# A hybrid four-mixer layer on one core: 44 transfers issued from GpSimd instead of ScalarE

## The chip, the cores and the metric

The kernel runs on one core of one Trainium2 chip. The metric is the device time in microseconds of one execution; the time before is the median of three runs. The engines are TensorE (PE in the profile, PEld for its weight loads), VectorE (DVE), ScalarE (ACT), GpSimd (POOL) and SyncE (SP). Transfers are issued from the queues of SyncE, ScalarE or GpSimd, and the same 16 DMA engines carry all of them.

## The reference

One pre-norm layer on x of 1 x 512 x 1024, float32. The input is normalised, multiplied with a combined input projection, and split into four causal token mixers of width 256 and four sets of gates:

```python
h = _rmsnorm(x, norm1_g)
proj = h @ w_in
p_gdn, p_lru, p_s5, p_rwkv, p_gate = _split(proj, (GDN_COLS, LRU_COLS, S5_COLS, RWKV_COLS, GATE_COLS))
ys = (_gdn_mixer(p_gdn, ...), _rglru_mixer(p_lru, ...), _s5_mixer(p_s5, ...), _rwkv7_mixer(p_rwkv, ...))
for i in range(N_BRANCH):
    term = jax.nn.sigmoid(gate_logits[:, :, i]) * (ys[i] @ w_branch[i])
    merged = term if merged is None else merged + term
x = x + (merged @ w_out).astype(x.dtype)
h2 = _rmsnorm(x, norm2_g)
x = x + (jnp.square(jax.nn.relu(h2 @ mlp_w1)) @ mlp_w2).astype(x.dtype)
```

A final norm closes it. Gated DeltaNet (GDN) and RWKV-7 are computed in chunks of 64 tokens, each with 4 heads; for both, a unit triangular 64 x 64 matrix has to be inverted for each of the 8 chunks and 4 heads. S5 is a diagonal complex recurrence over groups of 16 channels.

## The kernel before, in words

Every large product is made of three float32r products: each operand is split into a rounded part (hi) and the rest (lo). Weights come in units of 128 x 1024 (`unit`, line 316): SyncE loads `raw` (line 313), ScalarE makes hi (line 333), VectorE makes lo (line 334, which the profile shows as line 120 with tile lo). `proj` (line 415) is one 128 x 512 tile of the projection, 24 matmuls, tile acc.

The mixers are written as steps, and PLAN (line 68) lists them: among others rwkv_a, s5_a, s5_b, gdn_l, gdn_k, rwkv_b, s5_y, rwkv_i, gdn_b, gdn_i, rwkv_r, gdn_r, and between them the gates ga_10 to ga_31. After them come `merge` and `mlp`, which hold about half of the time. Each step runs at a priority level (LV, line 62). The order of instructions on each engine is then fixed at build time by a planner (`schedule_with_timeline_sim=True`, line 1834), which lays them out on a timeline of its own, by priority and by when their inputs are ready. Each engine works through its list in order. So the order on the engines follows from the engine that each instruction is given to, as well as from its place in the code. Buffers in SBUF are handed out by `al` (line 138) from a table of places (HOME), in the order of the code.

The places where ScalarE issues transfers:

- `tri_inverse` (line 444), run once for RWKV (scratch scrr) and once for GDN (scrg). The 16 pairs of 64 x 64 matrices are written to DRAM (line 448), read back as 128 groups of 16 x 16 diagonal blocks into `nb` (line 452), inverted there by VectorE in 15 steps (lines 457 to 461), written out as `tn` and its transpose `tm` (line 468) and read back in the matrix layout as `a0t` and `tf` (line 472). Each of the four exchanges is half SyncE's and half ScalarE's: two transfers (lines 448, 452) or four (468, 472). At 448 and 452 the halves are two parts of one tile, at 468 and 472 the first of a pair (tn, a0t) is SyncE's and the second (tm, tf) ScalarE's. TensorE then assembles the full inverse in the matmuls zp, t1p, t2p, z2p and z3p (tiles zpr to z3pr and zpg to z3pg): zp reads a0t, t1p reads tf. Each ScalarE transfer here has 1024 contiguous runs, of 64 or 256 bytes.
- `rwkv_a` (line 617): four transfers of 512 runs from kr to ab.
- `gdn_b` (line 864): four broadcast loads of 1024 runs from gscr into gr and br, beside four of SyncE's into eg.
- `s5_b` (line 1297): eight loads of 256 runs from scu into ug, read by the matmuls s5v.
- `s5_y` (line 1355): sixteen loads of 128 runs from scy into yf, which is then added, put through a GELU (ScalarE) and read by the matmuls glu.

These are 12, 4, 4, 8 and 16, together 44. ScalarE also issues four stores of the output in `finish` (line 1654). GpSimd issues 24 weight loads that add to what is there (lines 330 and 332), all after 350 us, and does the memsets.

Of the kernel before, what the change touches and what calls it, by code (L numbers as in the profile page):

```python
# [100 lines left out]
def trunk(ctx, tc, order, xT, wall, w8, prm, big, cst, gfr, out):  # L101
# [342 lines left out]
    def tri_inverse(nt, tf, nm):  # L444

        scr = tri_scr[nm]
        for par in range(2):
            (nc.sync, nc.scalar)[par].dma_start(
                out=flat(scr, 4160 * par, [[64, 64], [8320, 16], [1, 64]]), in_=nt[64 * par:64 * par + 64])
        nb, tn, tn2, tmp = (t1(n + nm) for n in ("nb", "tn", "tm", "tp"))  # L450
        for qe in range(2):
            (nc.sync, nc.scalar)[qe].dma_start(
                out=v3(nb, 16)[64 * qe:64 * qe + 64], in_=flat(scr, 1040 * qe, [[2080, 64], [64, 16], [1, 16]]))
        nb3, tn3, tm3, tp3 = v3(nb, 16), v3(tn, 16), v3(tn2, 16), v3(tmp, 16)
        V.memset(tn, 0.0)
        V.memset(tn[:, 0:256:17], 1.0)
        for j in range(14, -1, -1):
            n = 15 - j
            tt(V, tp3[:, 0:n, 0:n], tn3[:, j + 1:16, j + 1:16],
               nb3[:, j:j + 1, j + 1:16].to_broadcast([128, n, n]), MUL)  # L460
            V.tensor_reduce(out=tn3[:, j + 1:16, j:j + 1], in_=tp3[:, 0:n, 0:n], axis=AX.X, op=ADD)
        V.tensor_copy(out=tm3, in_=tn3.rearrange("p c r -> p r c"))
        fr(nb, tmp)
        t0t = t4("t0t" + nm)
        a0t = v3(t0t, 16)
        for qe in range(2):
            for s, t in ((0, tn3), (1, tm3)):
                (nc.sync, nc.scalar)[s].dma_start(
                    out=flat(tri_scr[nm, s], 1040 * qe, [[2080, 64], [64, 16], [1, 16]]), in_=t[64 * qe:64 * qe + 64])
        for par in range(2):  # L470
            for s, t in ((0, a0t), (1, tf)):
                (nc.sync, nc.scalar)[s].dma_start(
                    out=t[64 * par:64 * par + 64], in_=flat(tri_scr[nm, s], 4160 * par, [[64, 64], [8320, 16], [1, 64]]))
        fr(tn, tn2)


        zt, z2 = t4("zt" + nm), t2("z2" + nm)
        G.memset(zt, 0.0)
        zt3, z23 = v3(zt, 16), v3(z2, 16)
        hm = c_("hm")  # L480
        zp = ps("zp" + nm)
        zp4 = v4(zp, 16, 2)
        def pairs(t, x, r0, o):
            return t[r0:r0 + 64, x, :].rearrange("p (b c) -> p b c", b=2)[:, :, o:o + 16]
        for x in range(16):
            for r0 in (0, 64):
                mm(zp4[r0:r0 + 64, x], nt[r0:r0 + 64, x, :], pairs(a0t, x, r0, 0))
        for b in range(4):
            r0, c0 = 32 * b, 32 * (b % 2)
            if b % 2:  # L490
                ts(V, zt3[r0:r0 + 32, :, c0:c0 + 16], zp4[r0:r0 + 32, :, 1], hm[r0:r0 + 32, 0:1], MUL)
            else:
                act(zt3[r0:r0 + 32, :, c0:c0 + 16], zp4[r0:r0 + 32, :, 0], ACT.Copy, hm[r0:r0 + 32, 0:1])
        t1p, t2p = ps("t1p" + nm), ps("t2p" + nm)
        t1p4, t2p3 = v4(t1p, 16, 2), v3(t2p[:, 0:256], 16)
        for x in range(16):
            for r0 in (0, 64):
                mm(t1p4[r0:r0 + 64, x], zt3[r0:r0 + 64, x, :], pairs(tf, x, r0, 16))
        for x in range(16):
            for r0 in (0, 64):  # L500
                mm(t2p3[r0:r0 + 32, x, :], tf[r0:r0 + 32, x, 0:32], zt3[r0:r0 + 32, x, 0:16])
        for b in range(4):
            r0, c0 = 32 * b, 32 * (b % 2)
            A.copy(out=tf[r0:r0 + 16, :, c0 + 16:c0 + 32], in_=t1p4[r0:r0 + 16, :, b % 2])
            if b % 2 == 0:
                tt(V, a0t[r0:r0 + 32, :, 0:16], t2p3[r0:r0 + 32], a0t[r0:r0 + 32, :, 0:16], ADD)
        fr(zt)

        z2p, z3p = ps("z2p" + nm), ps("z3p" + nm)
        z2p3, z3p3 = v3(z2p, 16), v3(z3p, 16)  # L510
        for x in range(16):
            for par in range(2):
                r0 = 64 * par
                mm(z2p3[r0 + 32:r0 + 64, x, :], nt[r0:r0 + 32, x, 32:64], a0t[r0:r0 + 32, x, 0:32])
        for par in range(2):
            r0 = 64 * par
            if par:
                V.tensor_copy(out=z2[r0 + 32:r0 + 64], in_=z2p[r0 + 32:r0 + 64])
            else:
                A.copy(out=z2[r0 + 32:r0 + 64], in_=z2p[r0 + 32:r0 + 64])  # L520
        for x in range(16):
            for par in range(2):
                r0 = 64 * par
                mm(z3p3[r0:r0 + 32, x, :], z23[r0 + 32:r0 + 64, x, :], tf[r0 + 32:r0 + 64, x, 32:64])
        for par in range(2):
            r0 = 64 * par
            if par:
                V.tensor_copy(out=tf[r0:r0 + 32, :, 32:64], in_=z3p3[r0:r0 + 32])
            else:
                A.copy(out=tf[r0:r0 + 32, :, 32:64], in_=z3p3[r0:r0 + 32])  # L530

        fr(t0t, z2)
# [16 lines left out]
    def rwkv_a():  # L549
# [31 lines left out]
        for m in range(2):  # L581
            cl = slice(m * 128, m * 128 + 128)
            kf, sig, af, ei, ea = (t2(n) for n in ("kf", "sig", "af", "ei", "eia"))
            wt_ = al("wt", 520)
            wt = wt_.rearrange("p (c t) -> p c t", c=8)
            o = ps("wl")
            mm(o, b_("wup")[0:64, cl], wa[0:64])
            act(sig, o, ACT.Sigmoid, 1.0, p("w0", m))
            o = ps("al")
            mm(o, b_("wup")[64:128, cl], wa[64:128])  # L590
            act(af, o, ACT.Sigmoid, 1.0, p("a0", m))
            V.tensor_tensor_scan(out=sig, data0=reset, data1=sig, initial=0.0, op0=MUL, op1=ADD)
            V.memset(wt[:, :, 0:1], 1.0)
            act(wt[:, :, 1:65], v3(sig, 8), ACT.Exp, -KDEC)
            act(ei, sig, ACT.Exp, KDEC)
            tt(V, ea, ei, af, MUL)
            shifted(kf, 2 + m)
            sq = sig
            act(sq, kf, ACT.Square, p("kk", m))
            o = head_stat(sq, inv, "k")  # L600
            tt(V, ea, o, ea, MUL)

            act(af, af, ACT.Identity, p("ka", m), omu[:, 8 + m:9 + m])
            tt(V, af, af, kf, MUL)
            kp = af
            stt(kr[:, m, :, 0, :], v3(kf, 8), p("kk", m), wt[:, :, 0:64], MUL, MUL)
            stt(yk[:, m, :, 0, :], v3(kf, 8), p("kk", m), v3(ea, 8), MUL, MUL)
            tt(V, yk[:, m, :, 1, :], v3(kp, 8), v3(ei, 8), MUL)
            fr(kf, sig, ei, ea)
            rf, vf = t2("rf"), t2("vf")  # L610
            shifted(rf, m)
            tt(V, kr[:, m, :, 1, :], v3(rf, 8), wt[:, :, 1:65], MUL)
            for q in range(2):
                V.tensor_copy(out=wc[0:64, :, 2 * m + q], in_=wt[64 * q:64 * q + 64, :, 64])
            fr(wt_)
            for q in range(2):
                nc.scalar.dma_start(out=ab[0:64, :, 2 * m + q].rearrange("p c s t -> p c (s t)"),
                                    in_=kr[64 * q:64 * q + 64, m].rearrange("p c s t -> p c (s t)"))

            tt(V, rf, rf, kp, MUL)  # L620
            rb = al("rb", 128)
            act(rb, b64, ACT.Copy, p("rk", m))
            o = ps("bo")
            mm(o, rb, rf)
            fr(rb)
            shifted(vf, 4 + m)
            tt(V, rf, o, vf, MUL)
            bons.append(rf)

            for hf in range(2):  # L630
                o = ps("vT")
                for c in range(4):
                    mm(o[64:128, c * 128:c * 128 + 128], vf[:, (4 * hf + c) * 64:(4 * hf + c) * 64 + 64], cb)
                A.copy(out=sv[64:128, 4 * hf:4 * hf + 4, 2 * m:2 * m + 2, :], in_=v4(o[64:128], 4, 2))
            fr(af, vf)
# [190 lines left out]
    def gdn_b():  # L826
# [34 lines left out]
        for par in range(2):  # L861
            rr = slice(64 * par, 64 * par + 64)
            for s, t in ((0, gr), (1, br)):
                nc.scalar.dma_start(
                    out=v3(t, 16)[rr],
                    in_=scr[s * 16:s * 16 + 16, 64 * par:64 * par + 64].rearrange("(o x) i -> o x i", o=1).to_broadcast([64, 16, 64]),
                )
# [416 lines left out]
    def s5_b():  # L1284
# [9 lines left out]
        ug = t4("s5ug")  # L1294
        uf = scu.rearrange("m (g c) (t n) -> t c (m g) n", c=16, t=8)
        for t in range(8):
            nc.scalar.dma_start(out=v3(ug, 16)[16 * (7 - t):16 * (7 - t) + 16], in_=uf[t])
        ug3 = v3(ug, 16)
        H = t4("s5h")

# [35 lines left out]
    def s5_y():  # L1336
# [15 lines left out]
        yfv = yf.rearrange("p (m t n) -> p m t n", m=2, t=8)  # L1352
        for g in range(16):
            r0 = 16 * (g % 8)
            nc.scalar.dma_start(out=yfv[r0:r0 + 16, g // 8], in_=scy[:, :, g, :].rearrange("t c n -> c t n"))
        for m in range(2):
            sl = slice(m * 512, m * 512 + 512)
            stt(yf[:, sl], up[:, sl], p("sd", m), yf[:, sl], MUL, ADD)
# [481 lines left out]
```

## Time and profile before

| | |
|---|---|
| median of three runs | 871.31 us (868.24 to 874.57) |
| the profiled execution: its own time, its span | 874.06 us, 872.2 us |
| TensorE busy, mean granted clock | 853.8 us (98% of the span), 0.986 |
| VectorE, ScalarE, GpSimd busy | 550.1, 424.0, 28.3 us |
| ScalarE's queue: packets, MB | 23808, 6.16 |
| GpSimd's queue: packets, MB | 3456, 12.58 |

The mixers, with the gates and branches between them, take the span up to 484 us, where the first matmul of merge (oacc) starts; the MLP follows. In a row of the timeline the first two numbers are start and duration, then come engine, line, operation, and the tiles written and read (a tile's name in the trace may be its region, c, c1a or c1b). What stands in square brackets is the idle time of that engine just before the row and what ended it. A busy TensorE can be one whose clock has been lowered: the granted clock stands beside it in the table of stretches. ACTq, SPq and POOLq are the issuing queues; an issue from ScalarE or SyncE isn't counted as busy time of the engine, one from GpSimd is shown as a POOL row.

### The profile page before, as it was taken

The page shows a single profiled execution, that of the slowest core. Times are in us where ns is not written, and L with a number is a line of the kernel's source. Part 1 is how long each engine was busy: PE and PEld are TensorE (multiplying, and loading weights), DVE is VectorE, ACT ScalarE, POOL GpSimd, SP SyncE. Part 2 cuts the span into 40 slices and gives each one's busy share as a digit, 9 for nine tenths or more (in the row PEclk, how much of TensorE's full clock was granted, in tenths as well). Part 3 has the DMA queues.
Part 4 walks back from the last instruction along what each step waited for, and adds up shares of the span by engine and source line. Part 5 has one row for each costly group of instructions (what it writes and reads, how often), then busy time and mean ns, then how long its engine had stood idle before and what let it go on. Part 6 is the DMA issues. An engine that isn't in the chain of part 4 may idle for free.

```text
span 872.2 us, 12503 instructions
## 1 busy us (share of the span) xinstructions
PE 853.8 (98%) x4911; PEld 689.5 (79%) x4911; DVE 550.1 (63%) x978; ACT 424.0 (49%) x596; POOL 28.3 (3%) x40
## 2 busy tenths in 40 slices
PE   8999999999999999999999999999999999999996
PEld 7777877778777777778888788888888888888885
DVE  7899896984587358736655652464437553868553
ACT  7735648644533264434433334765545443644433
POOL 1000000000000000000000000000100110010000
PEclk9999999996999999999999999999999999999999
DMA  8434225276545652434223232557665777463302
GB/s 300 158 104 134 89 98 106 74 167 172 110 136 161 195 170 86 135 96 132 98 96 97 91 121 88 184 146 187 159 196 166 234 177 209 146 142 100 120 25 97
DMA packets 79292, 119.94 MB, mean 138 GB/s; under 512 B 42545, under 2 KB 49393, under 8 KB 79217
## 3 DMA queue, kind: packets, MB, share of 16 engines
q1 hardware_dynamic: 51968, 100.40, 36.2%
q0 software_dynamic: 3456, 12.58, 8.4%
q10 hardware_dynamic: 23808, 6.16, 3.6%
q8 instruction: 38, 0.62, 0.3%
q14 instruction: 22, 0.17, 0.1%
HBM read 103.79 MB, written 13.17 MB: 134 GB/s over the span
## 4 chain that ended last, share of the span: by engine, by line
PE 87%; DVE 5%; DMA 4%; ACT 2%; issue 1%; ACTq 0%; SPq 0%; DVEq 0%
PE acc L114 29%; PE facc L114 20%; PE dacc L114 17%; PE oacc L114 5%; PE bacc L114 5%; PE s5y L114 1%; DVE c L120 1%; PE s L114 1%; DVE lo L120 1%; DVE c L129 1%; DMA c1a<-scrg 1%; DVE c1b L120 1%; DMA scrr<-c1a 1%; PE s1g L114 0%; DMA c<-scrr 0%
## 5 line engine op out<-in xcount | busy, mean ns | idle before, releaser
L114 PE MATMUL acc<-c,hi 128*128 128x512 f32 x864 | 279.2, 402 | 2.0 <-ACT c L117 1.2
L333 ACT ACTIVATE hi<-raw 128x1024 fp32r<-128x1024 f32 x113 | 119.4, 1058 | 233.2 <-PE facc L114 73.6
L120 DVE TENSOR_TENSOR lo<-raw,hi 128x1024 fp32r<-128x1024 f32 x113 | 137.9, 1222 | 101.4 <-ACT hi L333 99.9
L114 PEld LDWEIGHTS acc<-c,hi 128*128 128x128 f32 x864 | 162.0, 190 | 39.1 <-issue 2.8
L114 PE MATMUL acc<-c,lo 128*128 128x512 f32 x432 | 171.9, 399 | 1.5 <-DVE lo L120 1.5
L114 PE MATMUL facc<-c,hi 128*128 128x512 f32 x336 | 103.5, 389 | 0.0
L114 PEld LDWEIGHTS acc<-c,lo 128*128 128x128 f32 x432 | 82.3, 190 | 21.1 <-DVE lo L120 2.4
L114 PEld LDWEIGHTS facc<-c,hi 128*128 128x128 f32 x336 | 63.1, 188 | 13.1
L117 ACT ACTIVATE c<-c 128x512 f32<-128x512 f32 (+5 forms) x101 | 63.9, 638 | 15.1 <-DVE c L120 11.1
L120 DVE TENSOR_TENSOR c<-c 128x16 f32<-128x16 f32 (+8 forms) x125 | 65.2, 536 | 3.7 <-ACT c L117 2.7
L114 PE MATMUL facc<-c,lo 128*128 128x512 f32 x168 | 65.6, 390 | 0.0
L114 PE MATMUL facc<-c,c1a 128*128 128x512 f32 x264 | 62.8, 391 | 0.0
L114 PE MATMUL dacc<-hi,c 128*128 128x512 f32 x176 | 57.4, 389 | 0.0
L114 PEld LDWEIGHTS facc<-c,c1a 128*128 128x128 f32 x264 | 49.3, 188 | 10.2
L117 ACT ACT_TABLE_LOAD x38 | 48.8, 1283 | 7.8 <-DMA c<-scy 4.3
L120 DVE TENSOR_TENSOR c1a<-raw,c1a 128x1024 fp32r<-128x1024 f32 x21 | 25.7, 1223 | 32.5 <-ACT c1a L333 32.4
L120 DVE TENSOR_TENSOR c<-acc,c 128x512 f32<-128x512 f32 x33 | 22.6, 689 | 34.3 <-PE acc L114 32.5
L114 PE MATMUL bacc<-c1a,hi 128*128 128x512 f32 x128 | 40.9, 405 | 0.7 <-DVE c L120 0.7
L333 ACT ACTIVATE c1a<-raw 128x1024 fp32r<-128x1024 f32 x21 | 22.2, 1059 | 36.4 <-PE facc L114 29.0
L114 PE MATMUL oacc<-c,hi 128*128 128x512 f32 x128 | 39.8, 392 | 0.1
L114 PEld LDWEIGHTS dacc<-hi,c 128*128 128x128 f32 x176 | 33.0, 188 | 6.9
L114 PEld LDWEIGHTS facc<-c,lo 128*128 128x128 f32 x168 | 31.5, 188 | 6.5
(398 smaller groups left out, 1193.7 us busy)
## 6 DMA issues: line engine op xcount, KB each, us to landing
raw<-in_wall_dram SPq DMA_DIRECT2D x134, 512.0 KB, 3.4
c<-in_wall_dram POOLq DMA_DIRECT2D x18, 512.0 KB, 5.5
c<-in_wall_dram SPq DMA_DIRECT2D x6, 512.0 KB, 3.2
raw<-in_wall_dram POOLq DMA_DIRECT2D x6, 512.0 KB, 5.7
scg<-c1b SPq DMA_DIRECT2D x11, 256.0 KB, 2.5
c<-scg SPq DMA_DIRECT2D x11, 256.0 KB, 3.9
c1b<-in_xT_dram SPq DMA_DIRECT2D x8, 256.0 KB, 5.5
c<-in_xT_dram SPq DMA_DIRECT2D x8, 256.0 KB, 4.5
```

Source lines behind the costliest of these rows:

```text
L114: P.matmul(out=o, lhsT=l, rhs=r, start=start, stop=stop)
L117: A.activation(out=o, in_=i, func=f, scale=scale, bias=bias)
L120: e.tensor_tensor(out=o, in0=a, in1=b, op=op)
L129: V.scalar_tensor_tensor(out=o, in0=a, scalar=s, in1=b, op0=op0, op1=op1)
L333: high.append(A.activation(out=hi, in_=raw, func=ACT.Copy, scale=1.0, bias=0.0).ins)
```

## The change

`G` is `nc.gpsimd`. At the places named above, every transfer that ScalarE issued is issued from GpSimd; SyncE's halves stay. The data, the shapes, the tiles and all other instructions are the same, and so are the four output stores.

```diff
-            (nc.sync, nc.scalar)[par].dma_start(
+            (nc.sync, G)[par].dma_start(
                 out=flat(scr, 4160 * par, [[64, 64], [8320, 16], [1, 64]]), in_=nt[64 * par:64 * par + 64])
...
-            (nc.sync, nc.scalar)[qe].dma_start(
+            (nc.sync, G)[qe].dma_start(
                 out=v3(nb, 16)[64 * qe:64 * qe + 64], in_=flat(scr, 1040 * qe, [[2080, 64], [64, 16], [1, 16]]))
...
-                (nc.sync, nc.scalar)[s].dma_start(
+                (nc.sync, G)[s].dma_start(
                     out=flat(tri_scr[nm, s], 1040 * qe, [[2080, 64], [64, 16], [1, 16]]), in_=t[64 * qe:64 * qe + 64])
...
-                (nc.sync, nc.scalar)[s].dma_start(
+                (nc.sync, G)[s].dma_start(
                     out=t[64 * par:64 * par + 64], in_=flat(tri_scr[nm, s], 4160 * par, [[64, 64], [8320, 16], [1, 64]]))
...
-                nc.scalar.dma_start(out=ab[0:64, :, 2 * m + q].rearrange("p c s t -> p c (s t)"),
+                G.dma_start(out=ab[0:64, :, 2 * m + q].rearrange("p c s t -> p c (s t)"),
                                     in_=kr[64 * q:64 * q + 64, m].rearrange("p c s t -> p c (s t)"))
...
-                nc.scalar.dma_start(
+                G.dma_start(
                     out=v3(t, 16)[rr],
...
-            nc.scalar.dma_start(out=v3(ug, 16)[16 * (7 - t):16 * (7 - t) + 16], in_=uf[t])
+            G.dma_start(out=v3(ug, 16)[16 * (7 - t):16 * (7 - t) + 16], in_=uf[t])
...
-            nc.scalar.dma_start(out=yfv[r0:r0 + 16, g // 8], in_=scy[:, :, g, :].rearrange("t c n -> c t n"))
+            G.dma_start(out=yfv[r0:r0 + 16, g // 8], in_=scy[:, :, g, :].rearrange("t c n -> c t n"))
```

## The prediction

> **What bounds the kernel now.** I read the page first, then the table of stretches, then the waits of TensorE, then the timeline around each moved transfer.
>
> ```profile
> PE 853.8 (98%) x4911; PEld 689.5 (79%) x4911; DVE 550.1 (63%) x978; ACT 424.0 (49%) x596; POOL 28.3 (3%) x40
> ...
> q0 software_dynamic: 3456, 12.58, 8.4%
> q10 hardware_dynamic: 23808, 6.16, 3.6%
> ```
>
> TensorE is busy for 853.8 of 872.2 us, so 18.4 us of idle time is all that a better order could win from waits. q10 is ScalarE's queue: counted from the code, its 48 transfers hold 23040 contiguous runs, and 16 closing packets for each make the 23808. 44 of them move (the four output stores stay). q0 is GpSimd's: 24 transfers of 128 runs and 16 packets each make 3456.
>
> The stretches (start:end, length, PE busy, PEld, DVE, ACT, POOL, clock, DMA share, GB/s):
>
> ```profile
> 140.00:160.00 20.00, 19.75 (x94) 15.26 (x94) 15.10 (x59) 19.49 (x26) 0.00 (x0) 1.00 0.46 89
> 200.00:220.00 20.00, 18.41 (x129) 16.02 (x129) 9.36 (x17) 9.19 (x15) 0.00 (x0) 0.66 0.74 200
> 220.00:240.00 20.00, 19.05 (x330) 14.95 (x330) 11.20 (x23) 12.72 (x19) 0.00 (x0) 0.91 0.50 102
> 820.00:872.00 52.00, 44.96 (x199) 36.89 (x197) 20.47 (x31) 19.36 (x35) 0.00 (x0) 0.96 0.19 67
> ```
>
> 7.0 of the 18.4 us lie in the last 52 us, where nothing moves. Around the moved transfers little is idle, but one thing costs more than idle time: between 200 and 240 us the granted clock is 0.66 and 0.91, worth up to (0.34 + 0.09) x 20 = 8.6 us.
>
> ```profile
> PE zpr L114 <- DMA c<-scrr: 1.6, 1, 1.6
> ...
> PE acc L114 <- ACT c L117: 1.2, 1, 1.2
> ...
> PE glu L114 <- ACT c L117: 1.0, 1, 1.0
> ...
> PE zpg L114 <- DMA c1a<-scrg: 0.7, 1, 0.7
> ```
>
> These are TensorE's own waits (total us, times, longest). Three hang on the moved code: zpr and zpg on SyncE's half of the inverses' loads, which share the 16 DMA engines with ScalarE's half, and glu, which comes at the end of the S5 output transfers.
>
> **The change part by part.** *ScalarE's side.* It loses 44 issues of 0.3 to 1 us. That frees ScalarE, not TensorE: ScalarE is 49% busy, and the waits above for it are 1.2 and 1.0 us, the second of which is really for the transfers before it. I take 0 (bounds: 0 and a gain of 1.2).
>
> *GpSimd's side.* What does one transfer of many runs cost there? The trace has only transfers of 128 runs (timeline of POOL, group of L330), beside the hardware queues at 128 and at 1024 runs:
>
> ```profile
> L330 POOL DMA_DIRECT2D c<-in_wall_dram x12 | 10.4, 864 | 124.1 <-DVE lo L120 80.9 <-DVE c1a L120 43.2
> 122.65 0.33 SPq L313 DMA_DIRECT2D raw<-in_wall_dram  x1
> 135.14 0.61 ACTq L448 DMA_DIRECT2D scrr<-c1a  x1
> ```
>
> So t, GpSimd's time for one transfer of 1024 runs, lies between 0.86 us (runs are free) and 8 x 0.864 = 6.9 us (all of the 0.864 goes with the runs). The hardware queue grows by 0.61/0.33 = 1.85, which would give 1.6. With ends so far apart I take the geometric mean, 2.4 us. Transfers of 128 runs cost 0.86. The Trainium skill, DMA: Bandwidth & Descriptors, section "Anatomy of one DMA — SWDGE (gpsimd) path", says that one can emit a lot of descriptors before the incremental cost shows up; no row here shows more than 128 runs, and by that rule t would stay near the low end (it has a rival below).
>
> *Early ones: four of 512 runs (L617) and eight of 256 (L1297).* Their data isn't used for long:
>
> ```profile
> 80.73 1.83 ACTq L1297 DMA_DIRECT2D c<-scu  x2
> ...
> 84.42 2.31 ACTq L1297 DMA_DIRECT2D c<-scu  x3
> 104.60 0.98 PE s5v L114 x28
> ...
> 239.87 0.45 PE L114 MATMUL r<-c,c 128*64 128x64 f32 x8
> ```
>
> Issue ends at 86.7 and the reader s5v comes at 104.6, 18 us later. Eight at most of 1.7 us (double of 0.86) from 80.7 end by 95. L617's are read by the recurrence, whose first matmul r comes at 239.9. Cost 0; if s5v came as soon as the data were there, the 8 us from 86.7 to 95 would count.
>
> *First exchange of RWKV's inverse (L448, L452).* One half of the matrix goes out and one half of nb comes back by GpSimd, each 1024 runs, the second after the first has landed. VectorE's recursion (L460) waits for both halves:
>
> ```profile
> 139.66 3.10 DMA c1b<-scrr
> 143.41 0.15 DVE L120 TENSOR_TENSOR c1b<-c,c1b 128x1 f32<-128x1 f32 x1
> 146.51 1.22 DVE L120 TENSOR_TENSOR lo<-raw,hi 128x1024 fp32r<-128x1024 f32 x1
> 148.40 0.69 DVE L120 TENSOR_TENSOR c1b<-c1b,c 128x512 f32<-128x512 f32 x1 [0.67 <-ACT c L117]
> 151.71 0.69 DVE L129 SCALAR_TENSOR_TENSOR c<-c,c1b 128x512 f32<-128x512 f32 x1 [1.66 <-ACT c L117]
> 154.19 0.90 DVE L120 TENSOR_TENSOR c<-c 128x512 f32<-128x512 f32 x3 [0.77 <-ACT c L117]
> ```
>
> Each leg grows by 2.4 - 0.61 = 1.8 us, so nb lands at 142.8 + 3.6 = 146.4 instead of 142.8. The recursion's first step, at 143.4, then waits 3.0 us, and behind it in VectorE's queue stands a lo split that TensorE needs. Later idle time (0.67 + 1.66 + 0.77 = 3.1 us) takes the delay back. TensorE loses between 0 (the planner writes the recursion later into the queue) and 3.0; I take half, **+1.5**.
>
> *Second exchange (L468, L472).*
>
> ```profile
> 191.04 1.19 POOL L478 MEMSET c1b<- 128x1024 f32 x1 [20.08 <-DVE c L461]
> ...
> 191.37 1.54 ACTq L468 DMA_DIRECT2D scrr<-c1b  x2
> 197.89 1.31 SPq L472 DMA_DIRECT2D c<-scrr  x2
> 201.85 0.30 PE L114 MATMUL zpr<-c,c1a 64*64 64x32 f32 x2 [1.59 <-DMA c<-scrr]
> 217.56 0.30 PE L114 MATMUL t1pr<-c,c1b 64*64 64x32 f32 x2
> ```
>
> With what the issues list has from issue to landing (KB each, median us):
>
> ```profile
> c<-scrr ACTq DMA_DIRECT2D x2, 256.0 KB, 7.6
> ...
> scrr<-c1b ACTq DMA_DIRECT2D x2, 64.0 KB, 6.0
> ```
>
> GpSimd's half fills tf, which is first read by t1pr at 217.6. Behind its own issue of about 0.7 us a ScalarE store landed after another 5.3 us and a load after 7.0: 191.4 + 4.8 + 5.3 + 4.8 + 7.0 = 213.3, so 4 us are spare. GpSimd's own list holds memsets only, here that of zt (L478); put behind the two stores it ends by 198, ahead of the zp matmuls whose results go into zt. SyncE's half fills a0t, for which zpr waits 1.6 us; today four transfers go out at once and take 6.5 us. If GpSimd feeds its two over 4.8 us instead of 1.5, SyncE's two get through sooner: **-1.6**, and by the same way **-0.7** at zpg. The half clock that follows I leave as it is: new waits can call such episodes as an old one can.
>
> *S5 output (L1355) and the gates of GDN (L864).*
>
> ```profile
> 217.50 0.81 ACTq L1355 DMA_DIRECT2D c<-scy  x2
> 225.38 4.30 ACTq L1355 DMA_DIRECT2D c<-scy  x9
> 232.17 1.31 ACTq L864 DMA_DIRECT2D c1a<-gscr  x2
> 234.48 0.96 ACTq L864 DMA_DIRECT2D c1a<-gscr  x1
> 234.49 1.98 PE L114 MATMUL glu<-c,c1a 128*128 128x512 f32 x4 [0.95 <-ACT c L117]
> 241.70 2.34 DVE L120 TENSOR_TENSOR c1a<-c1a,c 128x1024 f32<-128x1024 f32 x2
> 266.27 0.14 DVE L120 TENSOR_TENSOR c1a<-c,c1a 128x1 f32<-128x1 f32 x1
> ```
>
> ```profile
> c1a<-gscr ACTq DMA_DIRECT2D x4, 256.0 KB, 4.7
> ```
>
> The sixteen loads go from 217.5 to 229.7 now. GpSimd needs 16 x 0.86 = 13.8 us, to 231.3; a little of that it can gain at the start, where ScalarE was late, so I count 231.1, and glu waits **+1.4** more. Then four of 1024 runs: they start at 232.2, and gr is whole after three, 232.2 + 7.2 + 4 to land (4.7 less the issue) = 243.4, where VectorE wants it at 241.7: 1.7 us late. That reaches the second inverse: its recursion, at 266.3, is late by 1.7 and by the 3.6 of its own first exchange, 5.3 in all. VectorE stands still meanwhile with the recurrence of RWKV queued behind, while TensorE has projections; half again, **+2.7**.
>
> *Sum:* 0 + 1.5 - 1.6 - 0.7 + 1.4 + 2.7 = **+3.3 us**. The profiled execution took 874.06 (span 872.2 and 1.9 around it), 2.75 above the median of the runs; with +3.3 it would be 877.4, and the median 871.31 becomes **874.6 us**.
>
> **The rivals.** *Runs cost GpSimd dearly, slower.* With t near the upper end, the place is nb of both inverses. By the same steps at t = 4.5: RWKV (7.8 - 0.6)/2 = 3.6; GDN (7.8 + 8.0)/2 = 7.9; glu 1.4; tf, now short of its 4 us, 4.1; less 2.3: +14.7, or **886**. It decides (over 1%) from t = 3.7 on; at 5.0 it gives 890, at 6.9 some 904. For it: GpSimd is the one engine whose busy time shows descriptor work at all. Against: 128 runs cost only 0.5 us more than on SyncE's queue.
>
> *The half clock goes, faster.* If zpr no longer waits, the episode behind that wait may stay away: -8.6 - 2.3 + 1.4 = -9.5, **862**. For it: the clock fell just after the only wait of 1.6 us. Against: it fell a second time with no wait of TensorE there, and glu waits longer:
>
> ```profile
> 224.00:226.00 2.00, 2.00 (x6) 1.52 (x6) 0.80 (x2) 1.36 (x4) 0.00 (x0) 0.50 0.16 35
> ```
>
>  The Trainium skill, TensorE: Matmul & The Clock Gate, section "HAM oscillation — how this bites in real kernels", ties a halved clock to waits for DMA; the trace agrees for the first fall (0.66), not for the second (0.91).
>
> *All of it is hidden.* With t = 0.9 the inverses' exchanges hardly move and SyncE gains nothing either; only glu's 1.4 is left: **872.7**. This is what the skill's sentence on descriptors would give.
>
> **How the numbers follow.** My forecast has 0.37 (own range 870 to 879, both halves taken at 0 or whole), the dear runs 0.28, the hidden change 0.20, the clock 0.15. A measurement of this kernel tells about 1% (8.7 us) from nothing: faster by more, only the clock, 0.15; slower, only the dear runs, 0.28; within, 0.57. The range, 861 to 890, goes from the clock's case to t = 5.0.
>
> **What would show it.** Right: POOL rows of 2 to 3 us at L448 to L472 and 0.86 at L1355; VectorE idle some 3 us ahead of its first L460 step; zpr without a wait; glu waiting 2 us or more. Wrong in size: POOL rows under 1.2 us, or over 4. Wrong in kind: TensorE's order changed so that another wait, outside these places, holds most of the difference, or a span that differs where the waits don't, by the clock.

## The result, and the profile after

The changed kernel takes 883.07 us (median of four runs, 881.87 to 886.0) against 871.19 us of the kernel before beside it (868.24 to 874.57): ratio 1.0101, 95% interval 1.0057 to 1.0146. A few executions of these kernels run about 1% longer than the rest at a lower clock (one of 83 of the kernel before, two of twelve of e6 below); means and ratios leave them out. The profiled execution took 882.54 us (span 880.7, clock 0.983) where before had 874.06 (872.2, 0.986). The forecast was 874.6 in a range of 861 to 890: the time lies inside, 8.5 us above the forecast, and not for the reasons given. That it lies inside is luck: the upper half of the range was there for a GpSimd that is slow with many runs, and the next lines show that it isn't.

The page first (busy time; then packets, MB and share of each queue):

```profile
PE 859.6 (98%) x4911; PEld 691.5 (79%) x4911; DVE 549.8 (62%) x978; ACT 426.0 (48%) x597; POOL 57.4 (7%) x84
...
q0 software_dynamic: 5536, 17.70, 11.0%
q10 hardware_dynamic: 576, 1.05, 0.3%
```

The transfers did move: ScalarE's queue keeps the output stores, GpSimd's gains 5.1 MB. The 22528 runs that move (ScalarE's 23040 less the stores' 512) add only 2080 packets there (5536 - 3456). The groups of GpSimd give the price that the prediction could only bound:

```profile
L1355 POOL DMA_DIRECT2D c<-scy x16 | 8.4, 531 | 13.1 <-DMA scy<-c 13.1
L1297 POOL DMA_DIRECT2D c<-scu x8 | 4.5, 566 | 3.2 <-issue 3.2
L864 POOL DMA_DIRECT2D c1a<-gscr x4 | 3.3, 824 | 36.8 <-PE acc L114 22.1 <-DVE c1b L124 14.7
L617 POOL DMA_DIRECT2D c<-c1b x4 | 3.0, 752 | 74.2 <-DVE c L120 44.5 <-DVE wc L614 29.7
...
L448 POOL DMA_DIRECT2D scrr<-c1a x1 | 0.8, 843 | 8.3 <-DVE c1a L120 8.3
```

A transfer of 1024 runs (L448, L864) costs 0.83 us, not 2.4; one of 128 runs 0.53. So "Runs cost GpSimd dearly" is out, and by the prediction's own steps nearly nothing should have changed. Yet merge starts 8.55 us later (492.87 - 484.32). This is the timeline, before and after:

```profile
484.32 0.62 PE L114 MATMUL oacc<-c,hi 128*128 128x512 f32 x2
```

```profile
492.87 0.61 PE L114 MATMUL oacc<-c,hi 128*128 128x512 f32 x2
```

From there to the end both take the same (387.9 and 387.8 us). The difference lies in the mixers. There the lists of instructions differ: the planner has put TensorE's work in another order, and VectorE's. Laid side by side, the lists of the two traces differ in the place of 721 of TensorE's 4911 matmuls and of 221 of VectorE's 978 instructions. RWKV's inverse comes earlier (zpr starts at 185.2 us instead of 201.9), the S5 output later (glu at 255.5 instead of 234.5). TensorE's waits are other ones too (total us, times, longest):

```profile
PE acc L114 <- DVE c L120: 2.5, 2, 1.8
PE us L114 <- DVE c L528: 1.7, 1, 1.7
PE acc L114 <- ACT c L117: 1.6, 1, 1.6
...
PE zpr L114 <- DMA c<-scrr: 0.8, 1, 0.8
```

glu and zpg no longer wait. The largest new stall is two waits in a row, seen in the timelines of TensorE, ScalarE and VectorE (in brackets the idle time ahead of the row, and what ended it):

```profile
225.28 0.68 PE L114 MATMUL us<-c,c 64*64 64x64 f32 x8 [1.72 <-DVE c L528]
227.71 1.22 PE L114 MATMUL acc<-c,hi 128*128 128x512 f32 x2 [1.75 <-DVE c L120]
```

```profile
219.39 1.28 ACT L117 ACT_TABLE_LOAD   x1 [5.19 <-DMA c1a<-gscr]
```

```profile
221.78 2.73 DVE L120 TENSOR_TENSOR c<-c,c1a 64x256 f32<-64x256 f32 x7 [5.47 <-ACT c1a L117]
224.54 0.69 DVE L528 COPY c<-z3pr 32x512 f32<-32x512 f32 x1
```

ScalarE waits 5.19 us for the loads of eg ahead of its exp, VectorE 5.47 for that exp, and behind its seven products stands the copy of L528 that TensorE needs. In the kernel before, the products come at 232.2 us, and neither us nor acc waits behind them. The table of stretches shows the clock (third number from the end; before had 0.66 and 0.91 here):

```profile
200.00:220.00 20.00, 20.00 (x285) 17.98 (x284) 3.98 (x7) 7.71 (x14) 1.64 (x2) 0.74 0.50 133
220.00:240.00 20.00, 16.52 (x86) 13.03 (x85) 16.27 (x29) 13.22 (x18) 8.37 (x16) 0.83 0.39 123
```

The fall in the first of these stretches comes at 203 us, over 20 us ahead of the stall, with TensorE busy throughout.

### The profile page after: what moved, and what is told of

Its sections match the earlier page's. It is cut to its first block, busy times and chain, and to the rows that moved or that the text cites. A ratio compares the mean times of both kernels' runs of the same rounds, so it can differ in the third digit from the quotient of the medians.

```text
span 880.7 us, 12555 instructions
## 1 busy us (share of the span) xinstructions
PE 859.6 (98%) x4911; PEld 691.5 (79%) x4911; DVE 549.8 (62%) x978; ACT 426.0 (48%) x597; POOL 57.4 (7%) x84
## 3 DMA queue, kind: packets, MB, share of 16 engines
q0 software_dynamic: 5536, 17.70, 11.0%
## 4 chain that ended last, share of the span: by engine, by line
PE 87%; DVE 5%; ACT 3%; DMA 3%; issue 1%; SPq 0%; ACTq 0%; DVEq 0%
PE acc L114 30%; PE facc L114 20%; PE dacc L114 17%; PE oacc L114 5%; PE bacc L114 4%; DVE c L120 2%; ACT L117 1%; PE s L114 1%; DVE c L129 1%; DMA c1a<-gscr 1%; DVE lo L120 1%; PE s5y L114 1%; DMA c<-scrr 1%; DVE c1b L120 1%; DMA c1b<-in_xT_dram 1%
## 5 line engine op out<-in xcount | busy, mean ns | idle before, releaser
L114 PE MATMUL acc<-c,lo 128*128 128x512 f32 x432 | 175.4, 407 | 1.6 <-DVE lo L120 1.5
```

The source lines that it names most:

```text
L114: P.matmul(out=o, lhsT=l, rhs=r, start=start, stop=stop)
```

## The experiments

Theory ORDER: the transfers cost nothing on GpSimd; the planner's other order of everything else costs the time. Rival COST: transfers from GpSimd land later or disturb others, and that is the loss.

Besides medians and ratios I use one split of the time: **clock loss** = span x (1 - mean granted clock), and **the rest** = span x mean clock, that is work at full clock together with waits. Both are means over the runs of a kernel, and their sum is the span, to which the time adds 1.9 us. "merge" is the start of oacc in the profiled execution alone: e5 and e12 are one kernel, and theirs differ by 5.9 us. e1 to e4, e5 to e8 and e9 to e12 ran on three chips, each with the kernel before beside them (means of 874.0, 873.1 and 874.7 us), so the ratios are the safer comparison between them; the changed kernel was measured four times, in a session of its own.

| kernel | issue, order | runs | ratio to before (95%) | mean us | clock loss | the rest | merge |
|---|---|---|---|---|---|---|---|
| before | ScalarE, old | 82 | 1 | 873.9 | 8.6 | 863.4 | 484.3 |
| the changed kernel | GpSimd, new | 4 | 1.0101 (1.0057 to 1.0146) | 883.5 | 15.0 | 866.7 | 492.9 |
| e1 | GpSimd, old | 12 | 0.9973 (0.9943 to 1.0004) | 871.2 | 7.8 | 861.6 | 479.2 |
| e2 | ScalarE, new | 6 | 1.0148 (1.0112 to 1.0185) | 886.4 | 13.9 | 870.8 | 496.8 |
| e3 | halves swapped, planner's | 10 | 1.0084 (1.0052 to 1.0116) | 880.8 | 14.2 | 864.7 | 489.4 |
| e4 | GpSimd, new, three moved | 11 | 1.0068 (1.0041 to 1.0095) | 880.1 | 13.0 | 865.3 | 489.3 |
| e5 | GpSimd, old, L1355 in halves | 12 | 0.9926 (0.9898 to 0.9953) | 866.4 | 4.3 | 860.4 | 474.7 |
| e6 | GpSimd in quarters, old | 10 | 0.9981 (0.9948 to 1.0014) | 872.1 | 8.1 | 862.2 | 486.3 |
| e7 | inverses alone, planner's | 12 | 1.0021 (0.9990 to 1.0052) | 875.4 | 10.8 | 862.7 | 489.4 |
| e8 | the others alone, planner's | 6 | 1.0201 (1.0150 to 1.0253) | 891.3 | 24.0 | 865.5 | 500.8 |
| e9 | ScalarE, old, L1355 in halves | 12 | 0.9944 (0.9917 to 0.9970) | 869.9 | 5.6 | 862.5 | 478.6 |
| e10 | e5, GELU first | 12 | 0.9997 (0.9973 to 1.0021) | 874.0 | 9.6 | 862.7 | 483.1 |
| e11 | e5's transfers, planner's | 6 | 1.0133 (1.0084 to 1.0181) | 886.1 | 16.2 | 868.1 | 496.6 |
| e12 | e5 again | 11 | 0.9927 (0.9900 to 0.9954) | 868.5 | 6.3 | 860.4 | 480.6 |

### e1 and e2: engine and order taken apart

To hold an order, the list of each engine is written into the kernel, and each instruction is tied to the one ahead of it by a link that orders and makes no wait. e1 is the changed kernel with the lists of before; e2 the kernel before with the changed kernel's lists. The traces show that the lists were kept: VectorE's and ScalarE's are the same row for row in both pairs, and TensorE's but for three of 4911 matmuls in e1.

```diff
         mlp()
+    lay_out(tc, nc)
...
+def lay_out(tc, nc):
...
+    traced = {i.name: i for i in nc.cur_bb.bb.instructions}
+    info = mybir.DependencyInfo(mybir.DependencyClass.NoSync, mybir.DependencyReason.DATA)
...
+        for a, b in zip(line, line[1:]):
+            tc.add_manual_dep(b, a.name, info, reason="lay_out")
```

> The 44 transfers are issued from GpSimd, and every engine keeps the list of instructions that the kernel before has (written out in the code, so that the planner's choice plays no part). Theory ORDER (the transfers cost nothing on GpSimd, the planner's new order of the other instructions costs the 12 us): 867 to 875 us, zpr's wait of 1.6 us and the start of merge (oacc) near 484 us as before. Rival COST (transfers issued from GpSimd land later or disturb the others, and that costs the time): 878 us or more, merge at 490 or later, new waits of TensorE for scrr, scrg, gscr or scy.

> The 44 transfers are issued from ScalarE as before, and every engine keeps the list of the changed kernel. Theory ORDER: 879 to 887 us, with the stall of TensorE near 224 to 228 us (us waiting for c of L528, then acc for c) and a granted clock of about 0.5 behind it still there. Rival COST: 868 to 875 us, the stall gone or under 1 us.

Measured: 870.34 and 886.35 us, both where ORDER put them, and COST is refuted twice. Two details of ORDER missed in e1: zpr's wait is gone (it should have stayed), and merge starts at 479.2, not near 484. With the means of the table: the new order costs 12.5 us when ScalarE issues (873.9 to 886.4) and 12.3 when GpSimd does (871.2 to 883.5). Moving the issues *gains* 2.7 us in the old order and 2.9 in the new. That gain is at the edge of what was resolved (e1's interval ends at 1.0004), but has the same size in both orders. Could the links themselves cost time? e1 and e2 have them, before and the changed kernel don't. If engine, order and links add, the links' cost is half of (871.2 + 886.4) - (873.9 + 883.5), which is 0.1 us: nothing.

e1 is the kernel that the prediction had in mind, one in which only the engine changed. Its waits, and VectorE's first steps of the two recursions:

```profile
PE glu L114 <- ACT c L117: 3.9, 1, 3.9
```

```profile
201.59 0.30 PE L114 MATMUL zpr<-c,c1a 64*64 64x32 f32 x2 [0.18 <-DMA c<-scrr]
```

```profile
144.94 0.16 DVE L120 TENSOR_TENSOR c1b<-c,c1b 128x1 f32<-128x1 f32 x1 [0.29 <-DMA c1b<-scrr]
```

```profile
262.87 0.16 DVE L120 TENSOR_TENSOR c1a<-c,c1a 128x1 f32<-128x1 f32 x1 [0.27 <-DMA c1a<-scrg]
```

zpr's wait is gone as forecast, the recursions wait 0.3 us and not 3 to 5, and glu waits 2.9 us more. In e2 the stall named above is there but smaller: 1.1 us of us for L528, 1.8 of acc for c, and a clock of 0.69 at 228 to 232, not 0.5.

### e3: another order without any GpSimd

```diff
-                (nc.sync, nc.scalar)[s].dma_start(
+                (nc.scalar, nc.sync)[s].dma_start(
```

(and so in all four lines of `tri_inverse`).

> The kernel before, with the two halves of each exchange in the triangular inverses swapped between SyncE and ScalarE: as many transfers on each queue, none on GpSimd, and the planner lays out a new order (658 rows of TensorE stand elsewhere). Theory ORDER, in its wide form (any new order of the mixers moves the time by about 1% either way): outside 868 to 875 us, with no say on which side, and merge starting over 3 us away from 484. Against it (a new order alone is worth less than 0.4%): 868 to 875 us, merge at 481 to 487.

Measured: 880.21 us, merge at 489.4. A swap that leaves each queue its number of transfers costs 0.84%, nearly as much as the change did. zpr waits 3.3 us there. So a loss of this size needs no GpSimd. This run has no twin in the old order, so how much of it is the swap itself is open.

### e4: is the stall the loss?

```diff
 TensorE unchanged; VectorE:
-products x7, copy L528, addition to gr, product, eviction of acc
+copy L528, products x7, eviction of acc, addition to gr, product
 ScalarE:
-exp of eg, copies L530, L701, L702, L1346
+copies L530, L701, L702, L1346, exp of eg
```

> The changed kernel with its own order, but for three instructions: the copy of L528 stands ahead of the seven products that wait for eg, the eviction of acc that TensorE waits for stands ahead of the addition to gr, and ScalarE's exp of eg stands behind the four copies that it held up. Theory ORDER, with the stall at 224 to 228 us as its largest piece: TensorE's waits of 1.7 and 1.75 us there are gone, the half clock at 228 to 232 with them, so 3.5 + 2 or so less: 875 to 879 us. Rival (the stall is taken up by later slack, or the clock falls somewhere else): 881 us or more although the two waits are gone. Under COST the waits come back at the next reader of eg: 881 or more with waits of over 2 us at 228 to 235.

(This is a summary of the two engines' lists, no cut of code. The eviction of acc is VectorE's taking of a finished tile out of TensorE's accumulator.)

Measured: 879.37 us, 0.33% below the changed kernel (1.0068 against 1.0101), just over the band of the theory. The two intervals overlap, so that step is not resolved by the ratios. And the reason that I gave did not hold. us no longer waits, and acc now waits for both:

```profile
223.60 0.99 PE L114 MATMUL acc<-c,hi 128*128 128x512 f32 x2 [4.46 <-DVE c L120]
```

```profile
217.71 1.28 ACT L117 ACT_TABLE_LOAD   x1 [2.42 <-DMA c1a<-gscr]
```

The eviction still stands behind seven products that wait for eg. The half clock behind the wait stayed (0.59 at 224 to 228), while the fall at 200 to 220 did not come (clock 1.00 there, 0.74 in the changed kernel's profile). TensorE's list is the same in both kernels, matmul for matmul; first the changed kernel, then e4:

```profile
204.00:208.00 4.00, 4.00 (x76) 3.82 (x75) 0.40 (x1) 0.58 (x1) 0.00 (x0) 0.50 0.23 66
```

```profile
204.00:208.00 4.00, 4.00 (x65) 3.53 (x58) 1.67 (x3) 2.53 (x4) 0.00 (x0) 1.00 0.43 122
```

The stall as a cause of its own is not shown. That the three moved instructions gain something is likely and not resolved: the means lie 3.4 us apart, and 2.0 of that is clock loss.

### e7 and e8: do the parts add?

e7 changes only the four lines of `tri_inverse`, e8 only L617, L864, L1297 and L1355, each laid out by the planner.

> Only the four lines of the triangular inverses are changed (12 transfers on GpSimd), and the planner lays out its own order (660 lines of TensorE's list differ from before). Under COST the parts would add: this and e8 together about +12 us. Under ORDER each is a new order with a time of its own, outside 868 to 876 us as e3 was, and the two need not add up to the 12 us. If a new order is harmless after all and the whole change is needed for the loss: 868 to 876.

> Only L617, L864, L1297 and L1355 are changed (32 transfers on GpSimd), the inverses as before, the planner's own order (1091 lines of TensorE's list differ). COST: what e7 leaves of +12 us. ORDER: a time of its own, outside 868 to 876 us, not to be had from e7's by subtraction. Harmless order: 868 to 876.

Measured: 875.34 and 890.08 us. The whole change (+1.0%) is better than its larger part (+2.0%), so the loss is no sum of costs of transfers. e7 misses: its new order is nearly harmless (1.0021), so "every new order costs about 1%" is too strong. (e8's interval clears that of the whole change by little, 1.0150 against 1.0146.) e8 has TensorE wait 5.1 us in one place, and a low clock around it:

```profile
PE z2pr L114 <- DVE c L120: 5.1, 1, 5.1
```

```profile
200.00:220.00 20.00, 14.61 (x241) 12.69 (x240) 7.06 (x14) 8.59 (x15) 0.79 (x1) 0.70 0.53 133
220.00:240.00 20.00, 20.00 (x162) 17.22 (x163) 12.35 (x20) 9.20 (x13) 6.49 (x13) 0.70 0.41 120
...
320.00:340.00 20.00, 18.19 (x274) 15.01 (x269) 8.04 (x14) 13.01 (x23) 0.00 (x0) 0.66 0.21 64
```

The wait did not start the low clock. TensorE begins to wait at 211.6 us, and the clock had halved at 208.2, with TensorE busy:

```profile
208.00:210.00 2.00, 2.00 (x13) 2.00 (x13) 0.00 (x0) 0.00 (x0) 0.00 (x0) 0.54 0.61 183
```

```profile
216.72 2.27 PE L114 MATMUL z2pr<-c,c1a 32*32 32x32 f32 x64 [5.11 <-DVE c L120]
```

Of the 18 us that e8 loses, 16 are clock loss (24.0 against 7.9 of before beside it).

### e6: had a transfer cost 2.3 us

Each of GpSimd's transfers of 1024 runs is cut along its partitions:

```diff
+    def cuts(g):
+        return [(16 * i, 16) for i in range(4)] if g else [(0, 64)]
...
+            for i, w in cuts(par):
+                (nc.sync, G)[par].dma_start(
+                    out=flat(scr, 4160 * par + 64 * i, [[64, w], [8320, 16], [1, 64]]), in_=nt[64 * par + i:64 * par + i + w])
...
```

> As e1_gpsimd_old_order, but each of GpSimd's sixteen transfers of 1024 runs is cut into four of 256 runs (the same data): 4 x 0.57 = 2.3 us of GpSimd in place of 0.83, which is nearly the 2.4 us that the prediction assumed, in the old order that it assumed. If the prediction's steps hold (half of each delay of VectorE reaches TensorE): nb of RWKV's inverse 3 us later costs 1.5, gr and nb of GDN's inverse 5 to 6 us later cost 2.7 to 3, together 4 to 5 us over e1 (ratio to before 1.002 to 1.003). Rival SLACK (the idle time that VectorE has later takes the delay back, TensorE has other work meanwhile): under 1.5 us over e1, although VectorE waits 3 us ahead of its first step of L460.

Measured: a mean of 872.1 us, 0.9 over e1, which is less than the runs resolve. GpSimd's time came out as meant, the delay only in part:

```profile
135.74 2.23 POOL L452 DMA_DIRECT2D scrr<-c1a  x4 [9.71 <-DVE c1a L120]
140.60 2.23 POOL L457 DMA_DIRECT2D c1b<-scrr  x4 [2.63 <-DMA scrr<-c1a]
```

```profile
144.45 0.16 DVE L120 TENSOR_TENSOR c1b<-c,c1b 128x1 f32<-128x1 f32 x1 [0.59 <-DMA c1b<-scrr]
...
267.96 0.16 DVE L120 TENSOR_TENSOR c1a<-c,c1a 128x1 f32<-128x1 f32 x1 [2.32 <-DMA c1a<-scrg]
```

(With the cut, the code stands seven lines lower: L452 and L457 are L448 and L452.) nb of RWKV is there 0.6 us late instead of 3. That the first quarter travels while the next is prepared, so that issue time and landing time don't add, is argued and not shown. In GDN's inverse the wait is 2.3 us. The sixteen quarters of gr and br are not the reason, since GpSimd then stands idle for 23 us before the exchange; the exchange itself takes 2.2 us longer than in e1 (10.8 us from its first transfer on GpSimd to the recursion, 8.6 in e1). This one delay does reach TensorE. It waits for the copy of r (L700, here L707), which stands among the recursion's steps in VectorE's list, and in e1 it doesn't wait there:

```profile
PE us L114 <- DVE c1b L707: 1.8, 1, 1.8
```

So 1.8 of 2.3 us came through, more than the half that the prediction took, in one profile.

### e5, e9, e10, e11 and e12: a faster version

In e1 glu waits for the sixteen loads of L1355. From e1 to e5, and from before to e9:

```diff
-            G.dma_start(out=yfv[r0:r0 + 16, g // 8], in_=scy[:, :, g, :].rearrange("t c n -> c t n"))
+            (G, nc.sync)[g % 2].dma_start(out=yfv[r0:r0 + 16, g // 8], in_=scy[:, :, g, :].rearrange("t c n -> c t n"))
```

```diff
-            nc.scalar.dma_start(out=yfv[r0:r0 + 16, g // 8], in_=scy[:, :, g, :].rearrange("t c n -> c t n"))
+            (nc.scalar, nc.sync)[g % 2].dma_start(out=yfv[r0:r0 + 16, g // 8], in_=scy[:, :, g, :].rearrange("t c n -> c t n"))
```

Both keep the old order, with SyncE's eight behind its four loads of eg.

> As e1_gpsimd_old_order (all on GpSimd, the old order), but every second of the sixteen loads of L1355 is issued from SyncE, behind its four loads of eg. In e1 the sixteen take GpSimd from 216.1 to 225.2 us at 0.53 each and glu waits 3.9 us for the GELU behind them. Theory CHAIN (that run of issues sets glu's start): GpSimd's eight end near 220.4, SyncE's near 222, glu's wait falls under 1 us, and the time by 2 to 4 us against e1 (ratio to before 0.993 to 0.996). Rival (another wait, of eg or of gr, takes its place, or the clock falls there): as e1 within 1 us although glu's wait is short.

> e5_half_on_synce once more, beside e9 and e10 on one chip: ratio to before 0.990 to 0.996 if e5's gain is real; 0.997 or more if it was the draw of clocks in those runs.

Measured: 865.77 us, ratio 0.9926, and again 0.9927 (869.43 against 874.9 beside it). This beats both kernels. The chain is right in direction, not in size: glu was to wait under 1 us, and still waits 2.8 us in e5 and 3.3 in e12.

```profile
226.50 1.98 PE L114 MATMUL glu<-c,c1a 128*128 128x512 f32 x4 [2.79 <-ACT c L117]
```

```profile
200.00:220.00 20.00, 20.00 (x275) 17.18 (x277) 9.70 (x18) 9.43 (x19) 4.19 (x8) 1.00 0.79 216
220.00:240.00 20.00, 17.21 (x214) 12.13 (x214) 16.93 (x26) 14.09 (x16) 3.27 (x4) 1.00 0.53 144
```

Of the 3.8 us between e1's mean and that of e5 and e12 together (871.2 and 867.4 over 23 runs), the clock loss gives 2.6 (7.8 and 5.2) and the rest 1.2. The shorter chain can account for the rest; why the clock loss falls with it is not shown.

> The kernel before (ScalarE issues, old order), only that every second of the sixteen loads of L1355 is issued from SyncE behind its loads of eg, as in e5. Theory SPLIT (the gain of e5 is that the sixteen loads leave by two queues): 863 to 868 us, as e5. Rival ENGINE (the gain needs ScalarE freed of issues, which hold up its own copies and the table load ahead of the GELU): 869 to 874 us, with zpr's wait of about 1.6 us still there.

Measured: 869.35 us, ratio 0.9944. The time lies outside SPLIT's 863 to 868 and just inside ENGINE's 869 to 874, and yet ENGINE is not borne out: the halves alone, with ScalarE issuing, give 0.56% of e5's 0.73%, and zpr waits 0.9 us instead of 1.6.

```profile
PE glu L114 <- ACT c L117: 1.6, 1, 1.6
...
PE zpr L114 <- DMA c<-scrr: 0.9, 1, 0.9
```

Nor is glu's wait what is gained: it was 0.95 us in before. Of the 4.9 us to before on the same chip (874.7), the clock loss gives 3.7. The four kernels of the old order make a square: 873.9 (ScalarE, whole), 871.2 (GpSimd, whole), 869.9 (ScalarE, halves), 867.4 (GpSimd, halves). The halves gain 4.0 and 3.8 us, GpSimd 2.7 and 2.5. GpSimd's part stays at the edge: on one chip, e9 and e12 lie 1.4 us apart, which their runs don't resolve.

> As e5_half_on_synce, with ScalarE's GELU of yf ahead of its exp of eg. In e5 the GELU starts at 225.4, behind the exp and its table load, and its input is ready at 224.2; glu waits 2.8 us. If that order is what is left of glu's wait: 1.1 us less of it, 0 to 2 us less time than e5. Rival: the products that wait for eg come 2.5 to 3.4 us later and VectorE's list behind them with them (the additions to the GDN gates, an eviction of acc), so TensorE waits there: as e5 or up to 3 us more.

Measured: 873.83 us, ratio 0.9997, 0.7% above e5. The expectation fell, and the rival was right in kind and too small: glu's wait shortened by 0.8 us, but others came behind it, and the clock fell (at 227.7 us, 1.2 behind the end of glu's wait and ahead of the others):

```profile
232.87 2.92 PE L114 MATMUL s1g<-c 64*64 64x128 f32 x30 [1.11 <-DVE c L120]
```

```profile
220.00:240.00 20.00, 15.79 (x189) 10.27 (x188) 12.37 (x21) 10.43 (x11) 3.26 (x4) 0.69 0.46 115
```

> The same transfers on the same queues as e5 (all 44 moved off ScalarE, every second load of L1355 on SyncE), but the order of everything is the planner's own (1049 lines of TensorE's list differ from before). Theory ORDER: a time of its own, over 870 us, 5 us or more above e5, with merge later by as much. If the split itself is what counts: 863 to 869 as e5.

Measured: 886.89 us. With the planner's order the same queues that made the fastest kernel are 1.3% slower than before: 2.1% of difference by order alone (e12 beside it has 0.9927).

## Why the prediction was right and wrong, step by step

- **The order of work.** The failed step is the one that the prediction did not write out: its sum takes every engine's list as it was. Its last part names "TensorE's order changed so that another wait, outside these places, holds most of the difference" as being wrong in kind, and that is what came. By e1 and e2 the new order costs 12.3 to 12.5 us, the moved issues nothing (a gain of 2.7 to 2.9). It is not one wait that holds the difference, though: the largest new stall is 3.5 us, and e4 shows that it is not the whole cause.
- **"The half clock that follows I leave as it is."** Wrong in size. From before to after the mean clock loss grows by 6.4 us (8.6 to 15.0) and the rest by 3.3. Where only the order differs, the clock has about half of it: 5.3 of 12.5 us when ScalarE issues (8.6 to 13.9), 7.2 of 12.3 when GpSimd does (7.8 to 15.0). In e8 it is nearly all.
- **t = 2.4 us.** Mis-sized: 0.83 us for 1024 runs, under the low end of 0.86. The geometric mean between far ends was a poor choice; the row it started from (L330, 512 KB that are added to memory) was not like the transfers that moved. The sentence cited from the Trainium skill, DMA: Bandwidth & Descriptors, section "Anatomy of one DMA — SWDGE (gpsimd) path", fits: from 128 to 1024 runs GpSimd's time grows only from 0.53 to 0.83 us.
- **RWKV's first exchange +1.5, gates and GDN's inverse +2.7.** In e1 VectorE waits 0.29 and 0.27 us at the two recursions, and no wait of TensorE follows from either: 0 there, because of t. In e6, where GpSimd's time was made 2.2 us, 1.8 of 2.3 us of the second recursion's delay reached TensorE; the share of a half is thus no measured one, and too low in that profile.
- **Second exchange -1.6 and -0.7.** Right in e1: zpr waits 0.18 instead of 1.59, zpg not at all. The reason given, GpSimd's slower feed, was only argued, and the traces have another: in e1 GpSimd's two loads leave two microseconds behind SyncE's (200.0 and 198.0 us), where ScalarE's left 0.4 behind.
- **glu +1.4.** In e1 +2.9 (3.89 instead of 0.95). The sixteen issues took 8.4 us, not 13.8, but TensorE came earlier and waited.
- **ScalarE freed = 0.** Not settled alone. e1 and e5 show 2.5 to 2.7 us of gain for the whole move; e1's waits at zpr, zpg and glu sum to +0.8 (-1.4 - 0.7 + 2.9), so what gains lies outside them. By the means 0.8 us of it is clock loss (8.6 to 7.8), which the runs don't resolve.
- **The rivals.** "All of it is hidden" (872.7) is right for the transfers as such: e1 has 870.34 where before beside it has 874.22, so nothing is lost. "The half clock goes" (862) named the strongest lever, but for a reason that doesn't hold: in e1 zpr's wait is gone, and over twelve runs the clock loss is only 0.8 us smaller.

For a kernel over 1% slower the prediction had "only the dear runs", and those are refuted. So 874.6 came from terms that were too large, and the time from one that was missing; that the range held it is luck. What stays open: which of the planner's moves cost most, why it chose them, and what makes the clock fall in one order more than in another.

## What to carry to other kernels

Where a planner orders the instructions, a change of the issuing engine can change the whole schedule: hold the old order and run that too, before a cost is put down to the queue. A kernel whose TensorE is 98% busy can still lose 1 to 3% to the clock (8.6 us in before, 24.0 in e8), so compare clock loss and the rest apart, over several runs. Small transfers that end ahead of one reader can be worth spreading over two queues, even when each issue is cheap: here 4 us, most of it by the clock.

## What the runs showed of the hardware

- GpSimd's time per transfer hardly depends on the runs: 0.53 us (128 runs), 0.57 (256), 0.75 (512), 0.83 (1024). The 22528 runs went out from GpSimd in 1376 packets (2080 less 704 of 4 bytes, 16 for each of the 44 transfers), some 16 runs in each: by the packet sizes in the trace 1120 of 4096 bytes and 256 of 2048. On ScalarE's queue it was one packet for each run, of 64, 256 or 512 bytes.
- One kernel, 82 runs: 868.2 to 880.5 us, with clocks of 0.998 to 0.981. The clock loss of a run lies between 1.7 and 16.7 us, the rest between 860 and 868: most of the spread of 12 us is the clock, and a single profile doesn't show it.
- The clock's falls don't follow the length of TensorE's wait. It halved behind waits of 1.6 us (zpr, before), 2.0 (glu, e10), 3.3 (glu, e12), 3.9 (glu, e1) and 4.5 (acc, e4), and didn't behind 1.6 (glu, e9) and 2.8 (glu, e5). e5 and e12 are one kernel.
- It also falls with TensorE busy, for 9.79 us or more of the 10 us ahead: at 203 us in the changed kernel and in e2, at 223 in before, at 208 in e8, each time within 3 us of the last of t1pr and t2pr (126 small matmuls in 3.2 us). That work doesn't decide it: e1, e4, e5, e9, e10 and e12 run the same matmuls at full clock (1.00), e4 with the changed kernel's own list.
